# A new front input for an encoder block: weights and tokens in one stream, high parts before low parts, and an early load of the last weights

## The chip, the cores and the metric

The kernel runs on one core of a Trainium2 chip. The core has a matrix engine (TensorE, PE in the profile; its weight loads are the row PEld), three other compute engines (VectorE = DVE, ScalarE = ACT, GpSimd = POOL), and SyncE (SP), which here only issues loads and stores. Transfers between the chip's memory (HBM) and the core's own memory (SBUF) are carried by 16 DMA engines. Matrix products are added up in banks of a third memory, PSUM.

The metric is the device time of one execution in microseconds (us), less is better. Before the change the median of three runs is 951.37 us (951.23 to 951.52).

## The reference, cut to what matters

One layer of a bidirectional encoder, 256 tokens of width 2048, all in float32:

```python
h = _rmsnorm(x, norm1_g)
proj = h @ w_in                       # 2048 x 3072: q 1536 | k 512 | v 512 | u 512
a = _rmsnorm(_window_attention(q, k, v, sink), attn_out_g)
f = _rmsnorm(_fourier_mix(u, w_fourier), fourier_out_g)
x = x + jnp.concatenate([a, f], axis=-1) @ w_out
x = x + _conv_ffn(_rmsnorm(x, norm2_g), w_up, dw_w, dw_b, w_down)
return _rmsnorm(x, normf_g)
```

The feed-forward part has width 5504: an up-projection to gate and value, a depthwise convolution of width 3 and a GELU on the gate, and a down-projection.

## The kernel before, in words

**Products in two parts.** TensorE multiplies here in a reduced float32 format (F32R). To keep precision, each operand is split in a high part, which is the value rounded to that format, and a low part, which is the rest. A product is then three matmuls: high by high, high by low, low by high. ACT makes the high part of a weight tile (L182) and DVE the low part (L183). The same is done for the tokens, with the norm's gain g as a factor (`split_scaled`, L274 on ACT and L275 on DVE): one tile `hT[c]` holds, for each of four blocks of 128 channels, 256 columns of high parts and 256 of low parts.

**Units.** All weights come in units of 128 x 2048 floats (1 MB). A unit is loaded into one of three `raw` tiles by SP (L162), split into one of three `parts` tiles, and used by the matmuls. `split(i)` splits unit i and then issues the load of unit i + 3, so the `raw` tile that was just freed is refilled. In the main part unit i + 2 is split while unit i is multiplied (`step`). The order of the units is the order of the work: 4 units for u, 4 for v, 16 for q and k, 16 for the output projection, then those of the feed-forward part.

**The place of the parts.** `PLACES` (L148) says by how many floats the high and the low half are shifted inside the `parts` tile, for each way in which a unit is used: ("still": 0 and 16, "thirds": 0 and 32, "first": 16 and 16, and so on).

**The front.** Before the first matmul PE runs ten matmuls on a tile of ones (L267, `ps_warm`). Then comes u (the loop at L393): for each of 16 blocks k of 128 channels, the tokens of the block are split, a part of the weight unit is split, and six matmuls (`moving_weights`, L321 to L323) add to the two banks of `ps_u`, three for the first 128 tokens and then three for the others. In these matmuls the weights stream through the array (512 columns) and the tokens are loaded into it. The loads of the front are issued in the order of their use: the first u unit in four pieces of 256 KB, with pieces of the transposed tokens (`in_xT`) between them, the second in four, the third in two, the fourth in one. The norm's gain `vec[:, 0:16]` comes by a load that ACT issues. Then v: four units in the same manner as u, with the sums of squares of the tokens (`token_sums`), the Fourier products and other work beside them.

**q and k.** For each head's unit there are 32 matmuls into one bank (`still_weights`): here the weights are loaded into the array and the tokens stream. A high part of the weights meets high and low tokens at once (512 columns, L338), a low part meets the high tokens alone (256 columns, L340). The argument `lag=4` makes the order five highs, then low and high in turn, then five lows. In the feed-forward's up-projection the later units use `still_thirds` (L351), three matmuls of 256 columns for each block.

**The end.** The down-projection is done by products of blocks whose operands are sums; the sums of weights are built in a tile with the tag `sumw` (`first_sums`, by a DVE addition and by loads of POOL that add to what is there). The last such product is "N4" of the last set (its split is L950 on ACT and L951 on DVE). What is left over are the last three tiles of 128 rows of the down weights: four units of 768 KB, ("last", 0) to ("last", 3), one for each 512 output columns. `last_product(c, b)` makes the nine matmuls (L1205 to L1207) of columns c and tokens b, then `last_post` (an addition on DVE, L850; a sum of squares on ACT, L1069) and `gain` (POOL, L1076). Units 0 to 2 are split in the usual way; the fourth is split by `split_last(3)` (L1195 on ACT, L1196 on DVE) into tiles of its own, after `last_product(0, 0)`:

```python
    last_product(0, 0)
    split_last(3)
    for c in range(1, 4):
        last_product(c, 0)
```

The order on each engine is the order of this program; nothing reorders it.

Of the kernel before, what the change touches and what calls it, by code (L numbers as in the profile page):

```python
# [13 lines left out]
P = 128  # L14
D = 2048
S = 256
# [77 lines left out]
def block_kernel(  # L94
# [3 lines left out]
    xT: bass.AP,  # L98
# [29 lines left out]
    units = [(w_in[i], 2048, "first" if i < N_QK else "still") for i in range(24)]  # L128
# [19 lines left out]
    PLACES = {"still": (0, 16), "thirds": (0, 32), "first": (16, 16), "moving": (0, 0), "product": (28, 28)}  # L148
# [6 lines left out]
    def load(i, pieces=1):  # L155
        if i < len(units) and i not in raws:
            src, n, _ = units[i]
            raws[i] = wp.tile([P, 2048], F32, tag="raw", name=f"raw{i}", bufs=RAW)
            m = n // pieces
            for p in range(pieces):  # L160
                s = slice(p * m, (p + 1) * m)
                nc.sync.dma_start(raws[i][:, s], src[:, s])  # L162
                yield

    def split(i, pieces=1):

        for _ in split_parts(i, pieces):
            pass

    def split_parts(i, pieces):  # L170
        if i >= len(units):
            return
        _, n, place = units[i]
        raw = raws[i]
        hi, lo = halves[i] = parts_tile(f"parts{i}", place)
        m = n // pieces
        for p in range(pieces):
            s = slice(p * m, (p + 1) * m)
            if i == 0 and p == 0:
                nc.vector.tensor_copy(hi[:, s], raw[:, s])  # L180
            else:
                nc.scalar.activation(hi[:, s], raw[:, s], AF.Copy)  # L182
            nc.vector.tensor_tensor(lo[:, s], raw[:, s], f32(hi[:, s]), ALU.subtract)  # L183
            yield
        for _ in load(i + RAW):
            pass
        load_more(i + RAW)


    pa = ctx.enter_context(ExitStack())  # L190
    cat_pool = pa.enter_context(tc.tile_pool(name="cat", bufs=16))
    ph = pa.enter_context(tc.tile_pool(name="pa", bufs=1))

    hT = []
    vec = base.tile([P, V_N], F32, tag="vec", name="vec")
    xTc = [cat_pool.tile([P, 512], F32, tag="cat", name=f"xT{c}") for c in range(8)]
    chan = cat_pool.tile([P, 512], F32, tag="cat", name="chan")[:, 0 : 2 * P]
    wfs = cat_pool.tile([P, FW], F32, tag="cat", name="wfs")
    pos = cat_pool.tile([P, 2, S], F32, tag="cat", name="pos")
    Gs = [cat_pool.tile([P, FW], F32, tag="cat", name=f"G{c}") for c in range(2)]  # L200
    pos_hi = cat_pool.tile([P, 2, S], F32R, tag="cat", name="pos_hi")
    pos_lo = cat_pool.tile([P, 2, S], F32R, tag="cat", name="pos_lo")
    rel = cat_pool.tile([P, 512], F32, tag="cat", name="rel")
    xs = [base.tile([P, 2, 512], F32, tag=f"xs{c}", name=f"xs{c}") for c in range(4)]

    def load_x(c, o=0, n=512):
        nc.sync.dma_start(xTc[c][:, o : o + n], xT[:, c * 512 + o : c * 512 + o + n])

# [4 lines left out]

    first = load(0, 4)
    nc.scalar.dma_start(vec[:, 0:NK], vecs[:, 0:NK])
    load_x(0, 0, S)
    next(first)
    load_x(0, S, S)
    next(first)
    load_x(1)  # L220
    next(first)
    next(first)
    load_x(2)
    second = load(1, 4)
    next(second)
    next(second)
    load_x(3)
    next(second)
    next(second)
    load_x(4)  # L230
    for _ in second:
        pass
    third = load(2, 2)
    next(third)
    load_x(5)
    next(third)
    load_x(6)
    load_x(7)
    for _ in third:
        pass  # L240

    def load_more(i):

        if i == 4:
            for c in range(2):
                nc.sync.dma_start(xs[c], x[:, :, c * 512 : (c + 1) * 512])
        if i == 5:
            for c in range(2, 4):
                nc.sync.dma_start(xs[c], x[:, :, c * 512 : (c + 1) * 512])
        if i == 6:  # L250
            nc.sync.dma_start(chan, c_chan)
            nc.sync.dma_start(wfs, wf)
            nc.sync.dma_start(pos, c_pos)
        if i == 7:
            nc.sync.dma_start(vec[:, NK:V_N], vecs[:, NK:V_N])
            nc.sync.dma_start(rel, c_rel)

# [11 lines left out]
    def vcol(o, n=1):  # L269
        return vec[:, o : o + n]  # L270

    def split_scaled(dst, src, g):
# [4 lines left out]
        )  # L277

# [77 lines left out]
    def hk(k):  # L356
        return hT[k // 4][:, k % 4, :]

# [30 lines left out]
    for c in range(4):  # L389
        t = base.tile([P, 4, 512], F32R, tag=f"hT{c}", name=f"hT{c}")  # L390
        hT.append(t)
    ps_u = [bank(mm, f"ps_u{b}") for b in range(2)]
    for k in range(NK):  # L393
        c, q = k // 4, k % 4
        if q == 0:
            parts = split_parts(c, 4 if c < 2 else 2)
        split_scaled(hk(k), xTc[k // 2][:, (k % 2) * S : (k % 2 + 1) * S], vcol(V_G1 + k))
        next(parts, None)
        hi, lo = halves[c]
        for b in range(2):  # L400
            moving_weights(
                hi, lo, 512, [k], hk, b, ps_u[b], k == 0, k == NK - 1, q0=q
            )
        if q == 3:
            for _ in parts:
                pass
# [928 lines left out]
```

## Time and profile before

| what | value |
|---|---|
| median of three runs | 951.37 us |
| the profiled execution | 951.68 us, of which the span of the trace is 949.9 us |
| mean granted TensorE clock | 0.998 |
| PE busy | 937.8 us (99% of the span), 6277 matmuls |
| DVE busy | 711.7 us (75%) |
| ACT busy | 536.4 us (56%) |
| read from HBM | 211.80 MB, 225 GB/s over the span |

A page of the profile gives the busy time of each engine, the span in slices, the chain of work that ended last (followed back from the last instruction to whatever released each step), and the costliest groups of instructions. The trace behind it answers further questions: who waited for whom, the instructions in order of time, and busy times and DMA rates in any stretch. Line numbers (L321) are those of the kernel, and `out<-in` are the tiles written and read. A busy matmul's end is modelled: a matmul of 512 columns is shown as 0.39 us long, while the next one starts 0.227 us after it; so the distance between starts is what a matmul costs in a stream.

### The profile page before, as it was taken

Reading aid. Unit: us, or ns where it says so; the run is one execution under the profiler, and the core shown is the slowest. Engines: PE = TensorE matmul, PEld = TensorE weight load, DVE = VectorE, ACT = ScalarE, POOL = GpSimd, SP = SyncE. Lnnn points to the kernel's source line nnn. Section 1 sums busy time; section 2 is a strip of 40 time slices with the busy share of each in tenths; the row PEclk is TensorE's granted clock in tenths of the full one; section 3 lists DMA queues with packets and bytes.
Section 4 is the critical chain, followed back from the end, with each engine's and each line's share of the span. In section 5 each row is a group of like instructions: output and inputs, shape, how many; then the busy total and the mean of one; then the engine's idle time right before and its main releaser. Section 6 shows DMA issues by size and latency. Waiting matters only on the chain.

```text
span 949.9 us, 15032 instructions
## 1 busy us (share of the span) xinstructions
PE 937.8 (99%) x6277; PEld 856.6 (90%) x6277; DVE 711.7 (75%) x819; ACT 536.4 (56%) x623; POOL 47.2 (5%) x62
## 2 busy tenths in 40 slices
PE   8999999999999999999999999999999999999996
PEld 6788999888888999999999999999999999999984
DVE  5667878667667766769676887768878678888795
ACT  5846666644465555546555555555555556655544
POOL 0000000000000000000000000000000000000003
PEclk9999999999999999999999999999999999999999
DMA  8945444455559687677888779887787978779742
GB/s 308 355 177 177 141 171 137 174 177 177 180 207 299 206 262 218 191 256 216 272 239 254 247 244 268 259 265 227 260 240 238 300 243 266 247 211 273 223 156 89
DMA packets 33988, 214.87 MB, mean 226 GB/s; under 512 B 3840, under 2 KB 4352, under 8 KB 9472
## 3 DMA queue, kind: packets, MB, share of 16 engines
q1 hardware_dynamic: 29744, 184.54, 52.9%
q0 software_dynamic: 4032, 29.36, 16.6%
q8 instruction: 49, 0.80, 0.3%
q14 instruction: 19, 0.16, 0.0%
q10 hardware_dynamic: 144, 0.01, 0.0%
HBM read 211.80 MB, written 2.10 MB: 225 GB/s over the span
## 4 chain that ended last, share of the span: by engine, by line
PE 95%; DMA 2%; ACT 1%; DVE 1%; issue 0%; POOL 0%; SPq 0%; ACTq 0%; POOLq 0%
PE ps_val L351 22%; PE ps_gate L351 21%; PE ps_q L338 5%; PE ps_P L1059 3%; PE ps_P L1058 3%; PE ps_P L1057 3%; PE ps_N L1059 3%; PE ps_N L1058 3%; PE ps_N L1057 3%; PE ps_q L340 2%; PE ps_a L323 2%; PE ps_a L321 2%; PE ps_a L322 2%; PE ps_gate L338 2%; DMA raw<-in_w_in 2%; PE ps_val L338 2%
## 5 line engine op out<-in xcount | busy, mean ns | idle before, releaser
L183 DVE TENSOR_TENSOR parts<-raw,parts 128x2048 fp32r<-128x2048 f32 (+3 forms) x141 | 303.9, 2155 | 77.9 <-ACT parts L182 77.7
L182 ACT ACTIVATE parts<-raw 128x2048 fp32r<-128x2048 f32 (+3 forms) x140 | 254.4, 1817 | 85.8 <-PE ps_gate L351 19.9
L351 PEld LDWEIGHTS ps_val<-hU,parts 128*128 128x128 f32 x1824 | 211.6, 188 | 2.2
L351 PE MATMUL ps_val<-hU,parts 128*128 128x256 f32 x1824 | 212.9, 276 | 0.0
L351 PEld LDWEIGHTS ps_gate<-hU,parts 128*128 128x128 f32 x1776 | 206.4, 188 | 2.5
L351 PE MATMUL ps_gate<-hU,parts 128*128 128x256 f32 x1776 | 207.3, 276 | 0.0
L841 ACT ACTIVATE fa_v<-ps_val 128x256 f32<-128x256 f32 x38 | 14.6, 384 | 88.3 <-PE ps_val L351 88.2
L338 PE MATMUL ps_q<-hT,parts 128*128 128x512 f32 x192 | 61.3, 393 | 0.0
L951 DVE TENSOR_TENSOR parts_N<-sumw,parts_N 128x2048 fp32r<-128x2048 f32 x18 | 41.2, 2291 | 21.2 <-ACT parts_N L950 21.1
L1057 PE MATMUL ps_P<-parts_P,op_P 128*128 128x512 f32 x144 | 56.0, 389 | 0.0
L1058 PE MATMUL ps_P<-parts_P,op_P 128*128 128x512 f32 x144 | 56.0, 389 | 0.0
L1059 PE MATMUL ps_P<-parts_P,op_P 128*128 128x512 f32 x144 | 56.0, 389 | 0.0
L340 PE MATMUL ps_q<-hT,parts 128*128 128x256 f32 x192 | 45.5, 278 | 0.0
L950 ACT ACTIVATE parts_N<-sumw 128x2048 fp32r<-128x2048 f32 x18 | 34.4, 1913 | 14.3 <-PE ps_gate L351 10.6
L1057 PE MATMUL ps_N<-parts_N,op_N 128*128 128x512 f32 x108 | 42.0, 389 | 0.0
L1058 PE MATMUL ps_N<-parts_N,op_N 128*128 128x512 f32 x108 | 42.0, 389 | 0.0
L1059 PE MATMUL ps_N<-parts_N,op_N 128*128 128x512 f32 x108 | 42.0, 389 | 0.0
L338 PEld LDWEIGHTS ps_q<-hT,parts 128*128 128x128 f32 x192 | 35.2, 188 | 6.8
L321 PE MATMUL ps_a<-parts,cat 128*128 128x512 f32 x96 | 37.9, 394 | 0.0
L323 PE MATMUL ps_a<-parts,cat 128*128 128x512 f32 x96 | 37.5, 390 | 0.0
L322 PE MATMUL ps_a<-parts,cat 128*128 128x512 f32 x96 | 37.4, 389 | 0.0
L340 PEld LDWEIGHTS ps_q<-hT,parts 128*128 128x128 f32 x192 | 33.6, 188 | 1.0
(345 smaller groups left out, 1509.6 us busy)
## 6 DMA issues: line engine op xcount, KB each, us to landing
raw<-in_w_up SPq DMA_DIRECT2D x86, 1024.0 KB, 6.2
raw<-in_w_in SPq DMA_DIRECT2D x21, 1024.0 KB, 4.9
sumw<-in_w_down POOLq DMA_DIRECT2D x18, 1024.0 KB, 9.0
raw<-in_w_out SPq DMA_DIRECT2D x16, 1024.0 KB, 4.9
raw<-in_w_down_late SPq DMA_DIRECT2D x4, 1024.0 KB, 6.3
raw<-in_w_down_last SPq DMA_DIRECT2D x4, 768.0 KB, 4.4
raw<-in_w_in SPq DMA_DIRECT2D x8, 256.0 KB, 6.5
xs<-in_x SPq DMA_DIRECT2D x4, 512.0 KB, 10.1
```

What stands on the lines that cost most here:

```text
L182: nc.scalar.activation(hi[:, s], raw[:, s], AF.Copy)
L183: nc.vector.tensor_tensor(lo[:, s], raw[:, s], f32(hi[:, s]), ALU.subtract)
L321: nc.tensor.matmul(ps, ah, wh, start=first and q == q0, stop=False)
L322: nc.tensor.matmul(ps, al, wh, start=False, stop=False)
L323: nc.tensor.matmul(ps, ah, wl, start=False, stop=last and q == q0 + len(kk) - 1)
L338: nc.tensor.matmul(ps, hi[:, s], h, start=k == 0, stop=False)
L340: nc.tensor.matmul(ps[:, 0:S], lo[:, s], h[:, 0:S], start=False, stop=k == NK - 1)
L351: nc.tensor.matmul(ps[:, 0:S], w[:, s], h[:, o : o + S], start=k == 0 and n == 0, stop=k == NK - 1 and n == 2,)
L951: nc.vector.tensor_tensor(lo, src, f32(hi), ALU.subtract)
L1057: nc.tensor.matmul(ps, o[:, 0, p, :], hi[:, s], start=first and p == 0, stop=False)
L1058: nc.tensor.matmul(ps, o[:, 1, p, :], hi[:, s], start=False, stop=False)
L1059: nc.tensor.matmul(ps, o[:, 0, p, :], lo[:, s], start=False, stop=end)
```

## The change

Three things are changed.

1. **u's weights and tokens in one input.** The host lays out one array `u_in`: for each of the 128 partitions the 16 gains, and then for each block k the 256 tokens and the 512 weights of the block (768 floats). Nine loads bring it, of 1, 1, 1, 1, 2, 2, 2, 2 and 4 blocks, into one tile `u_raw` of a pool `front`, which is closed after u; the tiles of the attention part lie in its place afterwards. The u units are no longer units of `raw`, so the three `raw` tiles take the first three v units straight away; their loads, and those of the tokens in rows (`xs`), are issued behind the nine at the start. The loads `chan`, `wfs` and `pos` are issued once `front` is closed. For each load the tokens of its first block are split, then all the weights of the load in one piece, then the other tokens. The six matmuls of a block now take the two token halves in turn.
2. **q and k.** `lag=NK - 1`: sixteen highs, then sixteen lows; a new place "qk" with shifts of 16 and 32 floats.
3. **The last weights.** The unit ("last", 3) is not loaded into `raw` any more. Its load goes into the `sumw` tile, issued after the split of the last "N4"; `split_last(3)` now stands inside `last_product(0, 0)`, after the split of ("last", 2) and ahead of `last_post`.

The core of the diff:

```diff
-    units = [(w_in[i], 2048, "first" if i < N_QK else "still") for i in range(24)]
+    units = [(None, 2048, "first")] * N_V
+    units += [(w_in[i - N_V], 2048, "first" if i < N_QK else "qk") for i in range(N_V, 24)]
...
-    PLACES = {"still": (0, 16), "thirds": (0, 32), "first": (16, 16), "moving": (0, 0), "product": (28, 28)}
+    PLACES = {"qk": (16, 32), "still": (0, 16), "thirds": (0, 32), "first": (16, 16), "moving": (0, 0), "product": (28, 28)}
...
+    def load(i):
+
+        if i < len(units) - 1 and i not in raws:
             src, n, _ = units[i]
             raws[i] = wp.tile([P, 2048], F32, tag="raw", name=f"raw{i}", bufs=RAW)
+            nc.sync.dma_start(raws[i][:, 0:n], src)
...
+    KS = S + 512
+    front = ctx.enter_context(ExitStack())
+    fr = front.enter_context(tc.tile_pool(name="front", bufs=1))
+    u_raw = fr.tile([P, NK + NK * KS], F32, tag="u_raw", name="u_raw")
+    g1 = u_raw[:, 0:NK]
+
+    def load_u(k, n):
+        s = slice(NK + k * KS if k else 0, NK + (k + n) * KS)
+        nc.sync.dma_start(u_raw[:, s], u_in[:, s])
+
+    U_LOADS = [1, 1, 1, 1, 2, 2, 2, 2, 4]
+    for n, size in enumerate(U_LOADS):
+        load_u(sum(U_LOADS[:n]), size)
...
+    for i in range(RAW):
+        load(N_V + i)
+        for c in (0, 1) if i == 0 else (2, 3) if i == 1 else ():
+            nc.sync.dma_start(xs[c], x[:, :, c * 512 : (c + 1) * 512])
...
+    def u_weights(k, n):
+
+        if k % 4 == 0:
+            halves[k // 4] = parts_tile(f"parts{k // 4}", "first")
+        q = k % 4
+        hi, lo = (t[:, 512 * q : 512 * (q + n)] for t in halves[k // 4])
+        hi, lo = (t.rearrange("p (k f) -> p k f", f=512) for t in (hi, lo))
+        raw = u_raw[:, NK + k * KS : NK + (k + n) * KS]
+        raw = raw.rearrange("p (k f) -> p k f", f=KS)[:, :, S:KS]
+        if k == 0:
+            nc.vector.tensor_copy(hi, raw)
+            u_tokens(0)
+        else:
+            nc.scalar.activation(hi, raw, AF.Copy)
+        nc.vector.tensor_tensor(lo, raw, f32(hi), ALU.subtract)
+
+    def u_products(k):
+        hi, lo = (t[:, k % 4 * 512 : (k % 4 + 1) * 512] for t in halves[k // 4])
+        for n, (o, w) in enumerate([(0, hi), (S, hi), (0, lo)]):
+            for b in range(2):
+                a = hk(k)[:, o + b * P : o + (b + 1) * P]
+                nc.tensor.matmul(
+                    ps_u[b], a, w, start=k == 0 and n == 0, stop=k == NK - 1 and n == 2
+                )
+
+    k = 0
+    for size in U_LOADS:
+        if k:
+            u_tokens(k)
+        u_weights(k, size)
+        for q in range(size):
+            if q:
+                u_tokens(k + q)
+            u_products(k + q)
+        k += size
...
+    front.close()
...
-            still_weights(hi, lo, ps, range(NK), lag=4)
+            still_weights(hi, lo, ps, range(NK), lag=NK - 1)
...
-        elif p == "N4" and (g, c) != SETS[-1]:
+        elif (p, g, c) == ("N4", *SETS[-1]):
+            load_last()
+        elif p == "N4":
...
+    def load_last():
+        i = len(units) - 1
+        raws[i] = fp.tile([P, 2048], F32, tag="sumw", name=f"raw{i}", bufs=1)
+        nc.sync.dma_start(raws[i][:, 0 : units[i][1]], units[i][0])
...
         if (c, b) == (0, 0):
             ff_step(items.index(("last", 0)))
+            split_last(3)
         last_post(c, b, ps, o, n, part)
...
-    last_product(0, 0)
-    split_last(3)
-    for c in range(1, 4):
+    for c in range(4):
         last_product(c, 0)
```

`u_tokens(k)` is `split_scaled` of block k's tokens out of `u_raw`, with the gain out of the same tile. The loop over k at L393, the piecewise loads of the front and the load of `in_xT` are gone.

More of the change, by code (lines that the diff above doesn't have):

```diff
@@ L199, in block_kernel @@
[L199 to L203, printed above, removed]
+        raw = raws[i][:, 0:n]
+        hi, lo = (t[:, 0:n] for t in parts_tile(f"parts{i}", place))
+        nc.scalar.activation(hi, raw, AF.Copy)
@@ L386, in unit @@
         run(behind, i)
[L389 to L406, printed above, removed]
-            del halves[c]
     split(4)
```

128 lines of the change are left out of this document (44 added, 84 removed).

## The prediction

> **What bounds the kernel now.** I read the page first: the span and the chain of work that ended last, by engine.
>
> ```profile
> span 949.9 us, 15032 instructions
> ...
> PE 95%; DMA 2%; ACT 1%; DVE 1%; issue 0%; POOL 0%; SPq 0%; ACTq 0%; POOLq 0%
> ```
>
> PE is the bound: 95% of the chain is PE, and the rest is at the two ends. So a change counts only where it takes away time in which PE stands still, or alters the distance between two matmuls. The view of who waited for whom, for PE alone, says where it stands:
>
> ```profile
> PE ps_u L321 <- ACT parts L182: 1.1, 2, 0.7
> PE ps_e L1207 <- DVE lo L1196: 1.1, 1, 1.1
> PE ps_warm L267 <- POOL ones L259: 1.0, 1, 1.0
> PE ps_u L323 <- DVE parts L183: 0.5, 1, 0.5
> ```
>
> Only u at the start and `ps_e` at the end wait; between them, v, q, k and everything else have no wait. The ends of matmuls are modelled, so these sums are too small, and I take distances between starts from the timeline:
>
> ```profile
> 5.09 0.47 PE L321 MATMUL ps_u<-parts,hT 128*128 128x512 f32 x1
> ...
> 31.13 0.39 PE L321 MATMUL ps_v<-parts,hT 128*128 128x512 f32 x1
> ...
> 36.57 0.39 PE L321 MATMUL ps_v<-parts,hT 128*128 128x512 f32 x1
> ```
>
> From 31.13 to 36.57 there are the 24 matmuls of v's first unit: 0.227 us each. u has 96: 21.8 us at that pace, but took 31.13 − 5.09 = 26.04. So u loses 4.3 us. What u waited for is at the beginning of the chain, and in the DMA rate by stretch (last column; before it the DMA engines' busy share):
>
> ```profile
> 15.21 8.32 DMA raw<-in_w_in
> 23.64 1.07 ACT parts L182
> 24.74 1.24 DVE parts L183
> 26.02 0.50 PE ps_u L323
> ```
>
> ```profile
> 0.00:5.00 5.00, 4.00 (x20) 3.83 (x20) 0.99 (x4) 2.10 (x4) 0.88 (x8) 1.00 0.52 153
> 5.00:10.00 5.00, 3.85 (x14) 2.02 (x13) 2.25 (x5) 2.30 (x5) 0.00 (x0) 1.00 0.84 270
> 10.00:15.00 5.00, 5.00 (x20) 3.44 (x20) 3.54 (x7) 3.34 (x7) 0.00 (x0) 1.00 0.97 313
> 15.00:20.00 5.00, 4.64 (x19) 3.22 (x18) 3.78 (x7) 3.71 (x8) 0.00 (x0) 1.00 1.04 415
> ```
>
> u's last weights landed at 15.21 + 8.32 = 23.5 us, and PE resumed behind their low part at 26.02. The queue is full from 5 us on, yet for the first 15 us it moves 270 to 313 GB/s, and 415 after that. The first 15 us are the time in which the loads are small pieces; they are also simply the first 15 us. The trace does not tell these apart, and most of the forecast hangs on it.
>
> **The change, part 1: the front.** Bytes: 16 blocks of 128 × 768 floats are 6.3 MB, as much as before (4 u units and the transposed tokens), by 9 loads where there were 11 for the weights and 9 for the tokens. Durations from the groups by shape:
>
> ```profile
> L274 ACT ACTIVATE hT<-xT,vec 128x256 fp32r<-128x256 f32 x16 | 7.7, 498 | 2.3 <-DMA vec<-in_vecs 1.1 <-DMA xT<-in_xT 1.1
> L182 ACT ACTIVATE parts<-raw 128x2048 fp32r<-128x2048 f32 x2 | 3.8, 1915 | 2.7 <-PE ps_u L323 2.7
> L183 DVE TENSOR_TENSOR parts<-raw,parts 128x2048 fp32r<-128x2048 f32 x2 | 4.6, 2294 | 2.7 <-ACT parts L182 2.7
> ```
>
> Let T be the landing of the last load, blocks 12 to 15. ACT splits the tokens of block 12 (0.5 us) and then all 2048 weight columns in one piece (1.9), DVE follows with the low part (2.3): ready at T + 4.7. Of block 12's six matmuls four need no low weights; the last two restart PE (0.50 for the first, as at 26.02) and take 0.6 together, and the 18 of blocks 13 to 15 take 4.1. So u ends at T + 9.4, and never before 5.1 + 21.8 + some 0.3 = 27.2. Before, with 1024-column pieces and the tokens long there, it ended at T + 7.6 (23.5 to 31.1). So the coarser pieces cost 1.8 us, and the new front gains only if T comes before 21.7.
>
> The bounds of T. Late: the same bytes arrive as before, 23.5. Early: the first window as it was (0.77 MB by 5 us), the other 5.53 MB at 415 GB/s: 13.3 us, 18.3. I take a pace of 364 GB/s, the mean of the rows 10 to 15 and 15 to 20: 15.2 us, 20.2, and half a microsecond for the slowest DMA engine: T = 20.7. (Before, the rows add up to 6.3 MB moved at about 21.4, and the last load had landed 2.1 later.) Then u ends at 30.1: **−1.0 us**, between −3.4 (T 18.3) and +1.8 (T 23.5).
>
> A rule that speaks against the new layout: the Trainium skill, "DMA: Bandwidth & Descriptors", section "How a descriptor splits into AXI transactions", says that a read which doesn't start on a 256-byte boundary also fetches the bytes from the boundary below. A row of u_in is 49,216 bytes, 64 more than a multiple of 256, so three rows of four start off by 64 to 192 bytes. By an estimate from that page this adds 3% to a piece of 3 KB and under 1% to the last, some 0.2 us in all, and the sum would be 948.6; no run here shows it.
>
> What is moved beside that. The first matmul stays where the warm-up ends (5.09). The gain's load on ACT's queue goes; nothing stood behind it. The v and `xs` loads reach SP earlier but come in the same order of bytes behind u's, so they shift with T. `chan`, `wfs` and `pos` now wait on SP until the splits of u have read `u_raw` (T + 6 = 26.7); behind them in SP's queue stands v's fourth unit, which waits for the split of v's first unit anyway and isn't used for 16 us of v. POOL's queue issues nothing here. The token halves in turn cost nothing: the distance is 0.227 wherever the bank changes.
>
> **Part 2: q and k.** Same 512 matmuls. What can change is the distance between starts. Here are five lows in a row, and two units of the up-projection with matmuls of the same width:
>
> ```profile
> 69.37 0.76 PE L340 MATMUL ps_q<-hT,parts 128*128 128x256 f32 x5
> 69.96 0.38 PE L534 MATMUL ps_y<-uf,G 128*128 128x129 f32 x2
> ...
> 333.28 5.60 PE L351 MATMUL ps_gate<-hU,parts 128*128 128x256 f32 x48
> 338.72 5.60 PE L351 MATMUL ps_val<-hU,parts 128*128 128x256 f32 x48
> ```
>
> Five lows take 0.59, 118 ns each; the up-projection's 48 take 5.44, 113 ns each. Sixteen lows at 118 would be 0.08 us a unit over 113; for highs in a row I allow the same excess of 5 ns, another 0.08; less the 0.03 that five lows cost now, it is 0.13 × 16 = +2.1 us. The other end: the new shift of 32 floats is that of the up-projection's low half, whose rows run at 113; then the 0.02 of the five lows goes, and as much again if the five highs have it too: −0.3 to −0.7. I take the up-projection's row, the nearest with that shift: **−0.3 us**. Low parts are needed later than now, but no row of q or k waits for one, so that gains nothing.
>
> **Part 3: the end.**
>
> ```profile
> 929.41 0.39 PE L1207 MATMUL ps_e<-parts,act 128*128 128x512 f32 x1
> ...
> 931.64 0.50 PE L1207 MATMUL ps_e<-lo,act 128*128 128x512 f32 x1 [1.07 <-DVE lo L1196]
> 931.98 0.39 PE L1205 MATMUL ps_e<-hi,act 128*128 128x512 f32 x1
> ...
> 909.40 2.29 DVE L951 TENSOR_TENSOR parts_N<-sumw,parts_N 128x2048 fp32r<-128x2048 f32 x1
> ...
> 923.72 1.49 ACT L182 ACTIVATE parts<-raw 128x1536 fp32r<-128x1536 f32 x1 [3.95 <-PE ps_l L323]
> 925.24 1.76 DVE L183 TENSOR_TENSOR parts<-raw,parts 128x1536 fp32r<-128x1536 f32 x1
> ...
> raw<-in_w_down_last SPq DMA_DIRECT2D x4, 768.0 KB, 4.4
> ```
>
> From 929.41 to 931.98 PE starts four matmuls, 0.91 us at the stream's pace: 1.66 are lost to the fourth unit's split, which stands behind `last_post(0, 0)`. After the change its load is issued when N4's split is done (911.7) and lands 4.4 later, at 916. ACT starts its split behind that of ("last", 2) at 925.2 and ends at 926.7, DVE works from 927.0 to 928.8 (the durations of the two rows above, same shape), and PE is there at 929.6: ready 0.8 us ahead, so the whole 1.66 goes: **−1.7 us**. The price is that `last_post(0, 0)` moves on DVE from 926.9 to 928.8. Behind it wait ACT's sum of squares, POOL's gain and a `ps_e` bank that PE wants four products later; the later columns' sums decide, not this one. After it the chain is PE to the end, and the tail behind PE is unchanged.
>
> Sum: −1.0 − 0.3 − 1.7 = −3.0 us on a span of 949.9. The profiled execution took 951.68, 0.3 above the median, so I set it against the median: 951.37 − 3.0 = **948.4**.
>
> **The rivals.**
> - *Full pace at once.* The small pieces were the brake: T = 18.3, u ends at 27.7, −3.4. Time 951.37 − 3.4 − 0.3 − 1.7 = 946.0. For it: 20 loads become 9. Against it: the slow rows have a full queue (0.84 and 0.97). By the Trainium skill, "DMA: Bandwidth & Descriptors", section "Bandwidth", large transfers near 1 MB and over run best, and a transfer costs about 2 us and its bytes at 436 GB/s; an estimate from that would put T near 17 and the time at PE's floor for u, 945.5. The row after 15 us agrees with the pace, at 415.
> - *No earlier arrival.* The slow 15 us belong to the start of a run, whatever is loaded: T = 23.5, +1.8, and 951.37 + 1.8 − 0.3 − 1.7 = 951.2. The change then doesn't do what it says.
> - *A slower arrival (slower than before).* The pace of 270 GB/s lasts for all of u's bytes: 5 + 20.5, T = 25.5, u ends at 34.9, +3.8: 953.2. It decides from T = 23.7 on, where it has eaten the other two parts' 2.0. For it: rows grow longer but there are fewer loads in flight to even the DMA engines out. Against: the loads of tokens and u weights that fell after 15 us ran at 415 in the old pieces.
> - *Lows in a row stay slow.* +2.1 in place of −0.3: 950.8. The Trainium skill, "TensorE: Matmul & The Clock Gate", section "Step-by-step: what each phase is for", says that loading the next weights takes nothing from the running matmul; by that the order is worth 0 and the sum 948.7. The rows, 118 against 113, disagree.
>
> **How the numbers follow.** Forecast 0.38 (its own range 947.0 to 949.5), full pace 0.20, no earlier arrival 0.14, slower arrival 0.16, slow lows 0.12. The range goes from full pace with the best of part 2 (946.0 − 0.4, 945.6) to the slower arrival (953.2). A measurement can tell about 0.2%, 1.9 us, from no change. Below 949.5: the forecast but for 0.01, and full pace, 0.57. Above 953.3: half of the slower arrival and a little, 0.10. The rest, 0.33, is within.
>
> **What would show it.** Part 1: the first `ps_v` matmul near 30.1 (27.7 at full pace, 32.9 with no earlier arrival), a rate over 313 GB/s between 5 and 15 us, and a last wait of `ps_u` for DVE of some 0.5 to 1 us. Part 2: sixteen L340 matmuls in 1.81 us (1.89 if slow). Part 3: no wait of `ps_e` for L1196. The prediction is wrong if the rate of the first 15 us doesn't move or drops, or if v's units, which shift with u, begin to wait for their splits.

## The result, and the profile after

The changed kernel takes 947.80 us (median of 6 runs, 947.47 to 948.25), the kernel before, beside it on the same chip, 951.04 us (median of 6). The ratio is 0.9966, with a 95% interval of 0.9953 to 0.9979: a gain of 3.2 us or 0.34%, where the forecast was 3.0 (948.4 us). The sum came out; two of its three terms didn't, and they erred in opposite directions, so that the sum came out by luck.

The page of the changed kernel, the span and the chain of work that ended last by engine:

```profile
span 945.9 us, 15007 instructions
...
PE 96%; DMA 2%; SPq 0%; ACT 0%; DVE 0%; issue 0%; POOL 0%; ACTq 0%; POOLq 0%
```

The view of who waited for whom, PE alone (line, what it waited for, us in total, times, the longest):

```profile
PE ps_warm L209 <- POOL ones L201: 1.0, 1, 1.0
PE ps_u L253 <- ACT parts L241: 0.3, 1, 0.3
```

The wait of `ps_e` at the end is gone, and of the waits of `ps_u`, 1.6 us before, 0.3 is left. The stretches of the front (the last column is GB/s, the one before it the DMA engines' busy share) and the piece of the chain that is the last load of u:

```profile
0.00:5.00 5.00, 4.00 (x19) 4.01 (x20) 0.90 (x4) 2.04 (x4) 0.88 (x8) 1.00 0.66 215
5.00:10.00 5.00, 5.00 (x24) 4.04 (x24) 3.88 (x8) 3.35 (x7) 0.00 (x0) 1.00 1.01 368
10.00:15.00 5.00, 4.67 (x19) 3.23 (x19) 4.33 (x7) 4.95 (x9) 0.00 (x0) 1.00 1.04 434
15.00:20.00 5.00, 5.00 (x23) 4.14 (x23) 4.02 (x7) 3.14 (x6) 0.00 (x0) 1.00 1.00 425
```

```profile
4.74 14.22 DMA u_raw<-in_u_in
...
19.41 1.91 ACT parts L241
```

The last load of u landed at 4.74 + 14.22 = 18.97 us (by the exact times), 4.6 earlier than in the kernel before, and behind it, after the tokens of block 12, ACT splits all its 2048 columns in one piece, 1.91 us. Where the time went is read from the first matmul of each stage. From the timeline of the changed kernel (start, duration, line, tiles, count):

```profile
28.36 0.39 PE L338 MATMUL ps_v<-parts,hT 128*128 128x512 f32 x1
...
55.56 3.90 PE L355 MATMUL ps_k<-hT,parts 128*128 128x512 f32 x16
...
164.39 0.39 PE L338 MATMUL ps_a<-parts,cat 128*128 128x512 f32 x1
...
921.42 0.39 PE L1207 MATMUL ps_e<-parts,act 128*128 128x512 f32 x1
...
937.68 0.28 PE L1209 MATMUL ps_e<-lo,act 128*128 128x256 f32 x1
```

And the same places in the kernel before:

```profile
58.33 0.48 PE L338 MATMUL ps_k<-hT,parts 128*128 128x512 f32 x1
...
166.48 0.39 PE L321 MATMUL ps_a<-parts,cat 128*128 128x512 f32 x1
...
923.52 0.39 PE L1205 MATMUL ps_e<-parts,act 128*128 128x512 f32 x1
...
941.43 0.28 PE L1207 MATMUL ps_e<-lo,act 128*128 128x256 f32 x1
```

| place | before | after | difference | what the step added | forecast |
|---|---|---|---|---|---|
| first `ps_v` (u ends) | 31.13 | 28.36 | -2.77 | -2.77 (part 1) | -1.0 |
| first `ps_k` (v ends) | 58.33 | 55.56 | -2.77 | 0.00 | 0 |
| first `ps_a` (q and k end) | 166.48 | 164.39 | -2.09 | +0.68 (part 2) | -0.3 |
| first `ps_e` | 923.52 | 921.42 | -2.10 | 0.00 | 0 |
| last matmul | 941.43 | 937.68 | -3.75 | -1.66 (part 3) | -1.7 |
| end of the span | 949.9 | 945.9 | -4.0 | -0.24 (tail) | 0 |

So part 1 gave almost three times what I forecast, part 2 cost time where I had a small gain, and part 3 is right to a few hundredths. The tail behind the last matmul, from its start to the end of the span, was between 8.19 and 8.67 us in the traces of the experiments below, in which nothing behind it was changed, so I count its 0.24 for nothing. Without it the traces give -3.75; the medians give -3.2. The two traced executions are not the medians: the one before took 951.68 us, 0.6 over its median, the one after 947.65, 0.15 under. Parts 2 and 3 come out alike in the traces below (part 2 to 0.01 us, part 3 to 0.2), so what the medians lack is best looked for in part 1: by this estimate it is worth about 2.3 us in the medians (3.24 + 0.68 - 1.66), and 2.77 in this pair of traces.

### The profile page after: what moved, and what is told of

Same layout as the page of the kernel before. It is cut to its first block, busy times and chain, and to the rows that moved or that the text cites. A ratio compares the mean times of both kernels' runs of the same rounds, so it can differ in the third digit from the quotient of the medians.

```text
span 945.9 us, 15007 instructions
## 1 busy us (share of the span) xinstructions
PE 936.6 (99%) x6277; PEld 858.0 (91%) x6277; DVE 711.2 (75%) x816; ACT 535.7 (57%) x620; POOL 47.2 (5%) x62
## 4 chain that ended last, share of the span: by engine, by line
PE 96%; DMA 2%; SPq 0%; ACT 0%; DVE 0%; issue 0%; POOL 0%; ACTq 0%; POOLq 0%
PE ps_val L368 22%; PE ps_gate L368 21%; PE ps_q L355 5%; PE ps_P L1061 3%; PE ps_P L1060 3%; PE ps_P L1059 3%; PE ps_N L1060 3%; PE ps_N L1061 3%; PE ps_N L1059 3%; PE ps_q L357 2%; PE ps_a L340 2%; PE ps_a L338 2%; PE ps_a L339 2%; PE ps_gate L355 2%; PE ps_val L355 2%; PE ps_k L355 2%
## 5 line engine op out<-in xcount | busy, mean ns | idle before, releaser
L171 DVE TENSOR_TENSOR parts<-raw,parts 128x2048 fp32r<-128x2048 f32 (+1 forms) x129 | 293.4, 2274 | 70.8 <-ACT parts L170 70.6
L170 ACT ACTIVATE parts<-raw 128x2048 fp32r<-128x2048 f32 (+1 forms) x129 | 245.9, 1906 | 79.5 <-PE ps_gate L368 19.9
L355 PE MATMUL ps_q<-hT,parts 128*128 128x512 f32 x192 | 46.3, 393 | 0.0
L355 PEld LDWEIGHTS ps_q<-hT,parts 128*128 128x128 f32 x192 | 35.2, 188 | 6.9
L340 PE MATMUL ps_a<-parts,cat 128*128 128x512 f32 x96 | 37.5, 390 | 0.0
L946 DVE TENSOR_TENSOR parts_P<-sumw,parts_P 128x2048 fp32r<-128x2048 f32 x9 | 20.6, 2289 | 16.6 <-ACT parts_P L945 16.6
L355 PE MATMUL ps_gate<-hU,parts 128*128 128x512 f32 x96 | 32.7, 390 | 0.0
```

What stands on the lines that cost most here:

```text
L170: nc.scalar.activation(hi, raw, AF.Copy)
L171: nc.vector.tensor_tensor(lo, raw, f32(hi), ALU.subtract)
L340: nc.tensor.matmul(ps, ah, wl, start=False, stop=last and q == q0 + len(kk) - 1)
L355: nc.tensor.matmul(ps, hi[:, s], h, start=k == 0, stop=False)
L946: nc.vector.tensor_tensor(lo, src, f32(hi), ALU.subtract)
```

## The experiments

Each kernel is the changed one with the edit shown, except the last one of part 1, which is the kernel before with an edit. "T" is, as in the prediction, the landing of the last load of u.

### Part 2 undone, and part 3 undone

`e1_lag4`, the old order and shifts of q and k:

```diff
-"first" if i < N_QK else "qk") for i in range(N_V, 24)]
+"first" if i < N_QK else "still") for i in range(N_V, 24)]
...
-            still_weights(hi, lo, ps, range(NK), lag=NK - 1)
+            still_weights(hi, lo, ps, range(NK), lag=4)
```

> The changed kernel with part 2 undone: order of q and k as before (five highs, low and high in turn, five lows) and the shifts 0 and 16. In the two traces the stretch from the first matmul of k (ps_k) to the first of ps_a grew by 0.68 us with the change. Theory A (the order: a low matmul that follows a low matmul starts 118 ns after it, one that stands between highs 113 ns): this kernel wins that back, 947.8 - 0.7 = 947.1 us. Theory B (the stretch grew because q and k now run at another time beside other loads and splits, not by their own order): nothing is won back, 947.8.

Measured: 947.04 us (946.74 to 947.32), ratio to the kernel before 0.9955 (0.9943 to 0.9968). Its timeline:

```profile
55.31 0.48 PE L355 MATMUL ps_k<-hT,parts 128*128 128x512 f32 x1
...
163.46 0.39 PE L338 MATMUL ps_a<-parts,cat 128*128 128x512 f32 x1
```

From the first `ps_k` to the first `ps_a` it takes 108.15 us, the same as the kernel before (166.48 - 58.33) and 0.68 less than the changed kernel (164.39 - 55.56 = 108.83). Summed from first to last start, the sixteen units take 86.69 us here, 86.68 before, and 87.37 in the changed kernel. The loss is part 2's own, and Theory B falls. The other traces agree: the stretch takes 108.15 us wherever q and k have the old form, and 108.83 wherever they have the new one.

`e4_end`, the last weights in a `raw` tile again and their split after the first product:

```diff
-        if i < len(units) - 1 and i not in raws:
+        if i < len(units) and i not in raws:
...
-        elif (p, g, c) == ("N4", *SETS[-1]):
-            load_last()
-        elif p == "N4":
+        elif p == "N4" and (g, c) != SETS[-1]:
...
-            split_last(3)
         last_post(c, b, ps, o, n, part)
...
-    for c in range(4):
+    last_product(0, 0)
+    split_last(3)
+    for c in range(1, 4):
```

> The changed kernel with part 3 undone: the last weights are loaded into a raw tile in the usual order, and their split stands behind the first product's sums again. The prediction gave this part 1.7 us, and the two traces show 1.66 us less between the first ps_e matmul and the last one. Theory A (the split was the only wait and nothing else took its place): 947.8 + 1.7 = 949.5 us, and the wait of ps_e for the low part of about 1.1 us is back. Rival (the span after the first ps_e matmul is shorter for another reason, for example the tail of the stores, which is 0.25 us shorter in the changed kernel): 948 to 948.8 us.

Measured: 949.46 us (949.06 to 949.88), ratio 0.998 (0.9971 to 0.9989): 1.66 us more than the changed kernel, with the wait back:

```profile
PE ps_e L1207 <- DVE lo L1196: 1.1, 1, 1.1
```

Theory A holds, and the tail has no part in it.

### What makes the lows slow

In the changed kernel's timeline a unit of q, sixteen highs and sixteen lows (a group's duration goes from its first start to its last end; the last matmul is shown 0.39 or 0.28 long, so 15 distances are the duration less that):

```profile
101.92 3.79 PE L355 MATMUL ps_q<-hT,parts 128*128 128x512 f32 x16
105.55 2.05 PE L357 MATMUL ps_q<-hT,parts 128*128 128x256 f32 x16
```

(3.79 - 0.39) / 15 = 0.227 and (2.05 - 0.28) / 15 = 0.118 us: the highs run as fast as they ever do, the lows at 118 ns, as five lows in a row did before. In low and high in turn, most of the old units had 227 and 113. So I put highs and lows in turn throughout, `e2_lag0`:

```diff
-            still_weights(hi, lo, ps, range(NK), lag=NK - 1)
+            still_weights(hi, lo, ps, range(NK))
```

> The changed kernel with low and high in turn from the first block on in q and k; the shifts stay 16 and 32. In the feed-forward part units in this order take 5.327 us from first to last start, and the sixteen of q and k in the changed kernel take 87.37 us together. Theory A (the order): 16 x 5.33 = 85.2, and some 0.5 for units that start with a long first interval: 85.8, so 1.6 us less than the changed kernel, 946.2 us, and 0.9 less than with five highs ahead. Theory C (the shifts 16 and 32 slow the lows, whatever the order): lows stay at 118 ns, 16 x 16 x 0.0045 = 1.2 us of it isn't won, 947.4 or more.

Measured: 947.86 us (947.69 to 948.42), no gain at all. The sixteen units take 87.63 us. In its timeline, with the shifts 16 and 32, the two in turn:

```profile
101.76 0.39 PE L355 MATMUL ps_q<-hT,parts 128*128 128x512 f32 x1
101.99 0.28 PE L357 MATMUL ps_q<-hT,parts 128*128 128x256 f32 x1
102.11 0.39 PE L355 MATMUL ps_q<-hT,parts 128*128 128x512 f32 x1
```

That is 0.23 and 0.12 (229 and 117 ns on average over a unit): the order alone was not the cause, Theory A falls. Theory C, the shifts, gave 947.4 or more and 118 ns, and got both. So I tried order and shift in a mixture, each form in two of the sixteen units. `e3_mix` and `e5_mix2` differ from the changed kernel only in a table (shown here for the first) and the order that follows from it:

```diff
+    MIX = [
+        ("qk", "rows"), ("still", "rows"), ("thirds", "rows"), ("moving", "rows"),
+        ("qk", "strided"), ("qk", "thirds"), ("still", "turns"), ("qk", "twos"),
+    ]
...
-            still_weights(hi, lo, ps, range(NK), lag=NK - 1)
+            mixed(MIX[n % 8][1], hi, lo, ps)
```

> The changed kernel with eight forms of the q and k units, each used by two of the sixteen: (0) sixteen highs, then sixteen lows, shifts 16 and 32; (1) the same with shifts 0 and 16; (2) with 0 and 32; (3) with 0 and 0; (4) shifts 16 and 32, the lows in strides of four blocks, so that the tile of the tokens changes at each; (5) three matmuls of 256 columns for each block as in the up-projection, shifts 16 and 32; (6) low and high in turn, shifts 0 and 16; (7) two highs, then two lows, shifts 16 and 32. Read are the distances between starts, not the time. Theory A (what counts is that a low follows a low): 117 to 120 ns between lows in forms 0 to 4, 113 in form 6, in form 7 118 for the first low of two and 113 for the second; form 5, where a 256-column matmul follows another one too but with weights of the other half between, 113. Theory C (the shifts): one of forms 1 to 3 has its lows at 113, and form 5 has 118. Theory D (the addresses of the tokens): form 4 alone differs from form 0.

> The mixture of forms again, with other shifts of the high and the low half: sixteen highs, then sixteen lows with shifts (0) 16 and 16, (1) 16 and 48, (2) 32 and 32, (3) 8 and 8; low and high in turn with (4) 16 and 16, (6) 0 and 0; five highs ahead with (5) 16 and 16, (7) 0 and 32. Theory E (from the mixture before: lows in a row start 113 ns apart where the two shifts are alike or differ by 32, 118 to 120 where they differ by 16; highs in a row start 227 apart with the highs' shift at 16, 229 with it at 0): forms 0 and 1 have both, 227 and 113; form 2 has 229 and 113; form 3 has the lows at 113 and highs between. Rival F (the pace of the lows is set by what went before them, not by the shifts: highs that settled at 227 leave the lows at 118): forms 0 and 1 have 227 and 118, form 2 has 229 and 113.

Measured: the distances between starts in ns, averaged over a unit from the seventh matmul on (both units of a form agree within about 1).

| order | shifts high, low | highs | lows |
|---|---|---|---|
| rows (sixteen, then sixteen) | 16, 32 | 227 | 118 |
| rows, lows in strides of four blocks | 16, 32 | 228 | 118 |
| rows | 0, 16 | 229 | 120 |
| rows | 0, 32 | 229 | 114 |
| rows | 0, 0 | 229 | 113 |
| rows | 16, 16 | 227 | 120 |
| rows | 16, 48 | 227 | 120 |
| rows | 32, 32 | 233 | 114 |
| rows | 8, 8 | 234 | 117 |
| in turn | 16, 32 | 229 | 117 |
| in turn | 0, 16 | 232 | 118 |
| in turn | 16, 16 | 230 | 117 |
| in turn | 0, 0 | 233 | 120 |
| two and two | 16, 32 | 234 | 122 and 117 |
| five highs ahead | 0, 16 (before) | 227 | 113; 118 in the last lows |
| five highs ahead | 16, 16 | 237 | 117 |
| five highs ahead | 0, 32 | 229 | 117 |
| threes of 256 columns | 16, 32 | | 118 |

Units of the mixtures in the timeline, first 0 and 16, then 0 and 32, from `e3_mix`:

```profile
115.99 3.83 PE L385 MATMUL ps_q<-hT,parts 128*128 128x512 f32 x16
119.65 2.08 PE L387 MATMUL ps_q<-hT,parts 128*128 128x256 f32 x16
...
126.41 1.99 PE L387 MATMUL ps_q<-hT,parts 128*128 128x256 f32 x16
```

and 16 and 48 from `e5_mix2`:

```profile
119.74 2.09 PE L363 MATMUL ps_q<-hT,parts 128*128 128x256 f32 x16
```

What follows. Lows in a row can run at 113 (with 0 and 32, where 1.99 - 0.28 = 1.71 us is 15 distances of 114), so Theory A falls for the second time. Strided lows are as slow as the others: Theory D falls. Theory E, that like shifts give 113, falls with 16 and 16, which gives 120. Theory F, that the lows' pace follows from what ran before them, fits rows with the highs at 227 (lows 118 to 120) and at 229 or 233 (113 or 114), but not 0 and 16 (229 and 120) or 8 and 8 (234 and 117). Nor do order and shifts together settle it: in the kernel before, and in `e1_lag4` alike, the first and the third unit ran at 232 and 118 throughout and all the others at 227 and 113, with the same order and shifts. What the distance hangs on stays open. What is shown is its size, on average over a unit 113 to 122 ns for a low (122 is the first low of two and two) and 227 to 237 for a high, and that both the order and the two shifts move it. Of all forms in the table none is clearly faster over a unit than the one before the change; only rows with 0 and 0 come near (5.36 us from first to last start in the later unit, where the old form takes 5.35 to 5.37 in most of its units that don't begin with a long distance).

### Why u's data came earlier

`f1_cut` cuts each of the nine loads in its tokens and its weights, 18 loads with rows of 1 and 2 KB:

```diff
-        s = slice(NK + k * KS if k else 0, NK + (k + n) * KS)
-        nc.sync.dma_start(u_raw[:, s], u_in[:, s])
+        if k == 0:
+            nc.sync.dma_start(u_raw[:, 0 : NK + S], u_in[:, 0 : NK + S])
+        s = slice(NK + k * KS, NK + (k + n) * KS)
+        to, fr = (t[:, s].rearrange("p (k f) -> p k f", f=KS) for t in (u_raw, u_in))
+        for a, b in ((0, S), (S, KS))[k == 0 :]:
+            nc.sync.dma_start(to[:, :, a:b], fr[:, :, a:b])
```

> The changed kernel with each of the nine loads cut in two, the tokens (rows of 1 KB) and the weights (rows of 2 KB), 18 loads, the same input, order and bytes; splits and matmuls unchanged. Theory P (the small pieces were the brake: each row of 1 to 2 KB is moved at a lower rate than one of 3 KB or more): between 5 and 15 us some 270 to 320 GB/s as in the kernel before, and after 15 us too, T (the landing of the last u load) about 23, u ends at T + 9.4 = 32.4. Theory S (the first 15 us are slow by themselves, and the changed kernel is faster in them for another reason, its layout in memory): 368 and 434 GB/s as in the changed kernel, T 19, u ends at 28.4.

Measured: 950.59 us in one run. Its stretches from 5 to 20 us, and the last load in its chain:

```profile
5.00:10.00 5.00, 4.76 (x21) 3.49 (x21) 3.63 (x8) 3.07 (x7) 0.00 (x0) 1.00 0.99 306
10.00:15.00 5.00, 4.12 (x17) 2.76 (x16) 3.33 (x6) 3.75 (x7) 0.00 (x0) 1.00 1.07 383
15.00:20.00 5.00, 5.00 (x24) 4.14 (x23) 4.82 (x8) 4.07 (x7) 0.00 (x0) 1.00 1.07 375
```

```profile
11.26 10.50 DMA u_raw<-in_u_in
```

T is 21.76: cutting the loads gives back 2.8 of the 4.6 us. Theory S, with its T of 19, falls: the start isn't slow whatever is loaded. Theory P has the direction, but neither its 270 to 320 GB/s after 10 us nor its T of 23.

Part of the 2.8 is the length of the rows. A packet, one row that one DMA engine moves, took here 46 ns for 1 KB and 86 for 2 KB (medians up to T), and in the changed kernel 121 for 3 KB, 234 for 6 and 460 for 12. An estimate from these, with 16 engines that move packet after packet without a pause: 16.9 us for the rows of `f1_cut` and 15.0 for those of the changed kernel, 1.9 of the 2.8. The rest would be slow packets and a lag between the engines (see the last section); no run separates them.

`f2_pairs`, `U_LOADS = [2] * 8`:

> The changed kernel with eight loads of two blocks each. Theory P (small pieces are the brake): over 400 GB/s from 5 us on where the changed kernel has 368, T at 18.3 or earlier; the last piece is of two blocks, ready at about T + 2.8, so u's end is set by PE's own 21.8 us and a later start of the first matmul (its first load is twice as large, about 1 us later). Theory S (the start is slow whatever is loaded): 368 GB/s between 5 and 10 us again, T 19.

Measured: 948.06 us in one run. Between 5 and 10 us it moves 422 GB/s (368 in the changed kernel), and T is 18.56:

```profile
5.00:10.00 5.00, 3.68 (x17) 2.62 (x16) 4.25 (x7) 3.60 (x7) 0.00 (x0) 1.00 1.02 422
10.00:15.00 5.00, 5.00 (x24) 4.15 (x23) 5.00 (x9) 4.92 (x9) 0.00 (x0) 1.00 1.02 425
```

The first matmul comes 1.2 us later, and PE then waits another 1.0 for the low part, so nothing is won. Theory P holds here in the rate. Its T of 18.3 or earlier was missed, and 18.56 lies too near the 18.7 to 19.5 of the kernels with the changed kernel's loads to be called earlier from one run.

`f3_blocks` lays `u_in` out load by load, so that each load is one stretch of memory:

```diff
-        nc.sync.dma_start(u_raw[:, s], u_in[:, s])
+        u = u_in[:, P * s.start : P * s.stop].rearrange("o (p f) -> (o p) f", p=P)
+        nc.sync.dma_start(u_raw[:, s], u)
```

> The changed kernel with u_in laid out load by load, so that each of the nine loads reads one stretch of memory without gaps (in the changed kernel its rows lie 49,216 bytes apart). Theory P (the length of a row counts): nothing changes, T within 0.3 us of the changed kernel's 18.97. Theory L (the layout in memory counts, with the rows that start off by 64 to 192 bytes): T earlier, by 0.2 us or more.

Measured: 948.21 us in one run, T 19.50 by its chain:

```profile
4.61 14.90 DMA u_raw<-in_u_in
```

That is no earlier than in the changed kernel, or in five other kernels with the same front (18.7 to 19.2), so nothing speaks for Theory L. But T scatters by 0.5 us among those six, so a gain of 0.2 could not be seen in one run, and Theory P's "within 0.3 us" was missed as well.

`f5_pitch` is `f1_cut` with zeros behind each row of `u_in`, up to 16384 floats:

```diff
+            [tiles(inp["norm1_g"]), u_rows.reshape(P, -1),
+             np.zeros((P, 16384 - NK - NK * (S + FW)), np.float32)], axis=1),
```

> f1_cut again (18 loads, tokens and weights apart) with u_in padded so that its rows lie 65,536 bytes apart, a power of two, as all inputs' rows of the kernel before lie 8 or 16 KB apart. What is open is why the kernel before had T = 23.5 where f1_cut, with rows as small, had 21.76. Theory W (rows at a distance of a power of two are fetched more slowly): 270 and 313 GB/s between 5 and 15 us as before, T about 23.5. Rival (the distance of the rows is nothing, and the rest lies in the number, the order or the sizes of the twenty loads): T within 0.4 of 21.8, 306 and 383 GB/s.

Measured: 950.11 us in one run, 328 and 385 GB/s, and T at 21.35 by its chain:

```profile
10.88 10.46 DMA u_raw<-in_u_in
```

Theory W, with its T of 23.5, falls: at this distance, 64 KB, the power of two showed no cost.

`g1_whole` is the kernel before with u's second and third unit loaded whole:

```diff
-    second = load(1, 4)
-    next(second)
-    next(second)
-    load_x(3)
-    next(second)
-    next(second)
+    for _ in load(1):
+        pass
+    load_x(3)
     load_x(4)
...
-    third = load(2, 2)
-    next(third)
+    for _ in load(2):
+        pass
     load_x(5)
-    next(third)
```

> The kernel before with u's second and third weight unit loaded whole (1 MB with rows of 8 KB) where they came in four and in two pieces; the tokens' loads and their order between the weights, the input arrays and the splits stay. Thirteen u loads of weights and tokens fewer by four. Theory P (the pieces are the brake, whatever the array they come from): over 350 GB/s between 5 and 15 us where the kernel before has 270 and 313, the last u weights land at 21 to 22 in place of 23.5. Rival (the pieces cost nothing by themselves in the old layout, and the changed kernel's earlier landing comes from tokens and weights in one array): 23.2 to 23.8, 270 to 320 GB/s.

(It has 16 loads of tokens and weights in place of 20.) Measured: 951.88 us in one run. The stretches, and its first wait:

```profile
5.00:10.00 5.00, 4.54 (x15) 2.54 (x16) 3.22 (x6) 2.60 (x5) 0.00 (x0) 1.00 0.96 304
10.00:15.00 5.00, 2.89 (x11) 1.62 (x10) 1.51 (x4) 2.10 (x5) 0.00 (x0) 1.00 1.02 414
```

```profile
PE ps_u L313 <- ACT parts L182: 2.4, 2, 2.1
```

The last u weights land at 22.34 in place of 23.54, with 414 GB/s after 10 us where the kernel before has 313: the brake is there in the old layout too, and it eases with larger pieces. Theory P has the direction again, but 22.34 lies outside its 21 to 22 as well as outside the rival's 23.2 to 23.8, and its "over 350 GB/s" came after 10 us only. The time doesn't fall, because PE now waits 2.1 us for the 1 MB unit in the middle of u.

So the size of the early loads makes 2.8 us of the 4.6 from one side (`f1_cut`) and 1.2 from the other (`g1_whole`, where the first unit still comes in four pieces), each by one run. Size, number of loads and length of the rows were changed together, and only the share of the rows can be estimated. The kernel before was another 1.8 us later than `f1_cut`, with rows that are no shorter. Most of that is one lag: the first of the 16 DMA engines was done with the last load at 21.05 in the kernel before and at 20.62 in `f1_cut`, the last engine at 23.54 and 21.76. So 1.3 of the 1.8 is the wider lag of the slowest engine. Why it was wider stays open; `f5_pitch` speaks against the distance of the rows.

### A faster version

`b1_blocks` takes the old q and k (as in `e1_lag4`) and splits u's weights block by block, whatever the load's size:

```diff
-    k = 0
-    for size in U_LOADS:
-        if k:
-            u_tokens(k)
-        u_weights(k, size)
-        for q in range(size):
-            if q:
-                u_tokens(k + q)
-            u_products(k + q)
-        k += size
+    for k in range(NK):
+        if k:
+            u_tokens(k)
+        u_weights(k, 1)
+        u_products(k)
```

> The changed kernel with part 2 undone (as in e1_lag4, 947.04 us, where u ended at 28.1) and u's weights split block by block, whatever the size of the load. It tests the term T + 9.4: with pieces of 512 columns ACT needs 0.50 + 0.62 and DVE 0.48 + 0.69 us for a block, PE 1.36, so after the last landing at 19 nothing waits any more, and u ends at the start of the first matmul (4.8 to 5.1) + 21.8 + some 0.5 lost at the blocks 4 and 5 = 27.1 to 27.4. Theory A (the coarse pieces cost what the formula says): 947.04 - 0.8 = 946.2 us. Rival (u's end hangs on the landings, not on the pieces): 947.0.

`b2_blocks2` has `U_LOADS = [1, 1] + [2] * 7` beside that:

> As b1_blocks, with loads of 1, 1 and seven times 2 blocks. By the landings of the eight loads of two (5.42, 7.25, 9.14 and so on) the blocks 2 and 3 land at about 6.8, just in time for PE at 7.8, and 4 and 5 at 8.7, ahead of PE at 10.5: the loss at block 4 goes, another of 0.1 to 0.3 us may come at block 2. u ends at 27.0 to 27.3, 946.1 us; if the landing at block 2 is later, 946.4.

Measured: 946.25 us (945.83 to 946.34), ratio 0.9944 (0.9931 to 0.9958), and 946.43 us (945.96 to 946.97), ratio 0.9947 (0.9934 to 0.9959). In both PE waits for nothing in u any more. This is the timeline of `b1_blocks`:

```profile
5.28 22.57 PE L253 MATMUL ps_u<-parts,hT 128*128 128x512 f32 x96
27.69 0.39 PE L333 MATMUL ps_v<-parts,hT 128*128 128x512 f32 x1
```

u takes 22.41 us, 0.6 over the stream's 21.8, lost in the first distances. The only wait of PE that the view of `b1_blocks` shows is that of the warm-up:

```profile
PE ps_warm L209 <- POOL ones L201: 1.0, 1, 1.0
```

So Theory A holds: without the coarse pieces u's end no longer hangs on T, though it came 0.3 us behind the 27.1 to 27.4 that I expected, and in `b2_blocks2` 0.2 behind the 27.0 to 27.3. Against `e1_lag4` u ends 0.42 earlier by the traces, where the medians fall by 0.8; the first matmul happened to start 0.5 later in this one. In `b2_blocks2` u ends 0.19 earlier still, which the time doesn't show. Both beat the kernel before by 5 us and the changed one by 1.4 to 1.6.

## Why the prediction was right, point by point

**The bound.** Right: PE is 96% of the chain, and only the three places named have moved; the stages between them in the table kept their length to a hundredth of a microsecond. `chan`, `wfs`, `pos` and v's fourth unit, which I let wait at no cost, cost nothing: v ends 2.77 earlier, as u does.

**Part 1, "u ends at T + 9.4".** Right. In the changed kernel 18.97 + 9.4 = 28.37, measured 28.36; in six more kernels with the same nine loads and the same splits (T from 18.72 to 19.50) the distance was 9.38 to 9.43. So the 1.8 us that I gave to the coarser pieces were real, and taking them away (`b1_blocks`) brought u's end to 27.69, near the floor of 27.2.

**Part 1, T.** The term that was mis-sized, by 1.7 us: 18.97 for 20.7, and with it -2.77 for -1.0. The failing step is "I take a pace of 364 GB/s, the mean of the rows 10 to 15 and 15 to 20". That split the difference between a brake that stays and one that goes. In the runs it went when the larger loads came: 368 GB/s in the stretch in which the last single blocks came in, 434 and 425 afterwards, and 1.07 MB (5 us at 215) instead of 0.77 in the first 5 us. 1.07 + 1.84 + 2.17 MB are there at 15 us, the other 1.2 at 425 at 17.9, and the last landing came 1.1 behind that. The rival "full pace at once", with T 18.3, was nearest. What I held against it, that the slow rows have a full queue, was no argument: `f1_cut` has a share of 0.99 at 306 GB/s and `f2_pairs` 1.02 at 422.

By the Trainium skill, "DMA: Bandwidth & Descriptors", my estimate was a T near 17. It rests on a fit of 2 us and the bytes at 436 GB/s, which stands in that page's section "Anatomy of one DMA — SWDGE (gpsimd) path", not in "Bandwidth" as I had written, and which the page measured on loads that GpSimd issues; here SP issues them. The trace agrees with the 436 GB/s from 10 us on, with 434 and 425, and not before. The same page's section "How a descriptor splits into AXI transactions" led me to an estimate of 0.2 us for rows that start off a 256-byte boundary. In `f3_blocks` all rows but those of the first load start on one, and T is 0.5 later instead of 0.2 earlier. No run shows this cost here, and with a scatter of 0.5 in T none rules it out.

**Part 2.** Wrong in sign: +0.68 for -0.3. The failing step is "I take the up-projection's row, the nearest with that shift". The row matched in the shift of the low half alone. In the up-projection the high half has shift 0, here it has 16, and the order is another. With 0 and 32, lows in a row do run at 114 ns, as that row says; with 16 and 32 they run at 118, and so does the up-projection's own order. The rival "lows in a row stay slow" happened, at a third of its price: its +2.1 laid 5 ns on the highs as well, and those settle at 227. The sign of "sixteen L340 matmuls in 1.81 us (1.89 if slow)" was read right: 16 x 118 is 1.89. By the Trainium skill, "TensorE: Matmul & The Clock Gate", section "Step-by-step: what each phase is for", loading the next weights takes nothing from the running matmul; I concluded that the order is worth nothing. The runs disagree with my conclusion: the same 512 matmuls take 86.7 to 87.6 us in three orders and shifts. Whether the loading of the weights has a part in that, no run shows.

**Part 3.** Right: -1.66 for -1.7. The low part was to be ready 0.8 us ahead. In the changed kernel it is ready at 924.82 + 1.75 = 926.57 (the first row below), and PE takes up the fourth unit at 927.54, 0.97 later:

```profile
924.82 1.75 DVE L1198 TENSOR_TENSOR lo<-raw,hi 128x1536 fp32r<-128x1536 f32 x1
```

```profile
927.54 0.39 PE L1207 MATMUL ps_e<-hi,act 128*128 128x512 f32 x1
```

`last_post`, moved behind the split, held up nothing.

**The sum.** -1.0 - 0.3 - 1.7 = -3.0 came out within 0.3 of the medians, and that was luck. By the traces part 1 gave 1.8 more than forecast and part 2 1.0 less, so the sum is 0.75 short of their -3.75. The medians lie closer together than the two traced executions do, and so happen to lie closer to the forecast. The forecast put each of those two outcomes with a rival, and never both together.

## What to carry to other kernels

- Compare a forecast with the trace term by term, at the first matmul of each stage: a sum that comes out says little about its parts.
- A row prices an edit only where everything that may move it is alike. For matmuls here that is the order and the place of both operands. Where forms are cheap to mix, one kernel that uses each in two units measures them all.
- The size of a load and the size of the piece that is split from it are two choices. Large loads brought the data earlier; small splits let PE use it at once.

## What the runs showed of the hardware that was not expected

- **The slow start has no fixed end, and is mostly shorter with larger loads.** Single packets of u's loads took over 0.1 us more than others of their size: 108 of them in the kernel before, the last at 15.0 us; 77 in `f1_cut`, the last at 9.3; 65 in the changed kernel, the last at 8.9; 32 in `f2_pairs`, the last at 5.3. Behind that there were none up to 18 us, in rows of 1 and 2 KB too (`f1_cut`, 375 GB/s from 15 to 20 us). The loads alone don't decide it: `e3_mix`, with the very loads of the changed kernel, had such packets until 13.7. What ends this stretch stays open.
- **A load lands with its slowest engine, and a lag stays.** In the kernel before the first of the 16 DMA engines had finished u's last load at 21.05 and the last one at 23.54; from the load that landed at 17.76 on, the lag stayed at 2.5 us, load after load. In the changed kernel it was 18.25 to 18.97, a lag of 0.7.
- **The distance between matmuls depends on where their operands lie** and on the order of the matmuls: on average over a unit 113 to 122 ns for 256 columns and 227 to 237 for 512, at a granted clock of 1.00 in the windows. Two units of the same form can settle at different distances (227 and 113, or 232 and 118) and keep them.
